# Up product of an MLP: new order of the first two column pairs, new makers of their split operands, and two projections that take all attention heads at once

## The chip, the cores and the metric

The kernel runs on one core of a Trainium2 chip. The metric is the device time of one launch in microseconds (us), the median of several runs. The engines of a core work beside each other, each through a queue of its own in a fixed order: TensorE (PE, matmuls), VectorE (DVE), ScalarE (ACT), GpSimd (POOL), and SyncE (SP), which issues most of the transfers (DMAs); POOL issues some too.

## The reference, cut to what matters

One layer of a decoder with 1024 tokens and model width 1024. The change lies between the end of the cross-attention and the first part of the MLP:

```
h += CrossAttn(RMSNorm(h), RMSNorm(mem))     # 4 heads of 256, then the projection w_xo (1024 x 1024)
h += W_down( relu(RMSNorm(h) @ W_up)^2 )     # hidden width 4096
```

## The kernel before, in words

Everything is kept transposed: a tile has 128 channels as partitions and the 1024 tokens as its free dimension. The hidden state h is eight such tiles, ht0 to ht7. Matmuls of float32 values are made of three: each operand is split in a high part (a rounded cast, made by ACT) and a low part (the value less its high part, made by DVE or POOL), and high x high, high x low and low x high are added up in PSUM. In the profile, `oh`/`ol` and `wh`/`wl` are such halves, and nearly every matmul has line L73, that of a helper.

**Projection of the attention.** The outputs of heads 0 and 1 are four split tiles, parts0; those of heads 2 and 3 are parts1. `project` (L1345) multiplies four of them with a 128-column piece of w_xo (24 matmuls into a PSUM tile `ps_g`, of which there are two) and DVE adds the result to an ht tile (L1350). Ahead of the MLP stage all eight tiles get the part of parts0 (L1360 to L1362), while the last pieces of the attention (`values`, PSUM tile `ps_xo`) are worked in between; work that is put off with `after` runs at `step` calls between matmuls, or all at once at `drain`.

**Stream tiles of the up product.** A stage of its own (L1404 to L1437) starts with the spread of the norm's factor over all partitions: DVE makes a diagonal matrix `hx_dg` (L242), PE multiplies it (`ps_bs`), ACT copies the result to `rbx`. Then for kp = 0 to 3 the tiles i = kp and kp + 4 get the projection of parts1, are written out (`d_h`, by SP), and are scaled into v (L1419). From the two v tiles, cut in halves of 512 tokens, seven stream operands of a Strassen-like scheme are made (x11, t1, t2, x21, x22, t3, t4), each split by `slice_of` (L1383) in a cast on ACT (L1386) and a subtraction on DVE (L1387). In the profile they are `blk`. They take memory that others leave, in the order that `spare` yields (L1368): of the split tiles of earlier stages, of the ht tiles, and at last of pool `opd`, tag `sl`, in which the v tiles, rbx and hx_dg lie (four places). `next` of a place whose tile is still read waits for its readers.

**The up product.** Class `Pair` (L1468): 16 pairs of column blocks of w_up, seven products for each instead of eight, 12 matmuls each (four k x three), 1344 in all, into PSUM tiles `ps_up` of a pool with four banks. `weights(j)` makes the stationary operand `st` of product j out of the loaded w_up tiles (`ws`) or sums of them (`s`, on DVE): a cast on ACT (L1449), a subtraction on POOL (L1450). `result` adds the products up: p1 is ACT's copy of product 1, u2 = p1 + product 6 (L1526), u5 = u2 + product 5 (L1529); product 7 is added to u2 in L1531, and the outputs r are u2 + product 5, u2 + product 4, u5 + product 3 and p1 + product 2, then squared where positive, and written out. The bank of product 5 is read for the last time after product 7.

Pairs 0 and 1 form the first group (L1545): (0,1), (0,5), (1,1), (1,5), then products 6, 2, 3, 7, 4 of pair 0, and the same of pair 1. In (pr, j), pr is the pair and j the product. The weights of a whole group are emitted ahead of its products, at high priority; each engine's final order is made by a scheduler from the emitted order and these priorities. Behind the up product stands the down product (`ps_d`).

Of the kernel before, what the change touches and what calls it, by code (L numbers as in the profile page):

```python
# [17 lines left out]
P = 128  # L18
# [37 lines left out]
def trunk_kernel(tc, w_io):  # L56
# [3 lines left out]
    with ctx:  # L60
# [1144 lines left out]
        with ExitStack() as sc:  # L1205
# [136 lines left out]
                ):  # L1342
                    after(start + at, lambda fn=fn, args=args: fn(*args))

            def project(parts, slot, i2, j):  # L1345
                wh, wl = last_slot[0] = slot
                cols = lambda w, k: w[:, k * 256 + j * P:k * 256 + j * P + P]
                ps = gemm_ch(lambda k: (cols(wh, k), cols(wl, k)), hi(parts), lo(parts), 4, T)
                hv = ht[i2 * 2 + j]
                dve.tensor_add(hv, hv, ps)  # L1350

            last_slot = [None]
            parts0 = [pair(opb) for _ in range(4)]
            parts1 = []
            for h in range(4):
# [1 line left out]
                if h == 3:  # L1357
                    parts1 += [pair(opa) for _ in range(4)]
                attend(h, qT, parts0[h * 2:] if h < 2 else parts1, h % 2 * 2 if h > 1 else 0, 8)
            for i2 in range(4):  # L1360
                project(parts0, wslot(w_io["w_xo"][0, i2]), i2, 0)
                project(parts0, last_slot[0], i2, 1)  # L1362
            drain()

        def spare():  # L1368

            for pool_, tags, n in ((opc, ("oh", "ol"), 4), (opb, ("oh", "ol"), 4), (opd, ("sl",), 1)):  # L1370
                for tag in tags:
                    for _ in range(n):
                        yield pool_, tag
            for i in (0, 4, 1, 5, 2, 6, 3, 7):
                yield hp, f"ht{i}"
            for _ in range(3):
                yield opd, "sl"

        opd = ctx.enter_context(tc.tile_pool(name="opd", bufs=4))
        spares = spare()  # L1380
        blocks = {}

        def slice_of(name, src):  # L1383
            pool_, tag = next(spares)
            t = pool_.tile([P, 2, 512], F32R, tag=tag, name="blk")
            act.copy(t[:, 0, :], src)  # L1386
            dve.tensor_sub(t[:, 1, :], src, t[:, 0, :].bitcast(F32))  # L1387
            blocks.setdefault(name, []).append(t)

        f = []  # L1390
# [13 lines left out]
        with ExitStack() as sc:  # L1404
# [5 lines left out]
            for kp in range(4):  # L1410
                if kp % 2 == 0:
                    slots = [wslot(w_io["w_xo"][1, kp // 2 + 2 * q]) for q in range(2)]
                vs = []
                for q in range(2):
                    i = kp + 4 * q
                    project(parts1, slots[q], i // 2, kp % 2)
                    nc.sync.dma_start(d_h[i], ht[i])
                    v = opd.tile([P, T], F32, tag="sl", name="v")
                    dve.scalar_tensor_tensor(v, ht[i], C("g_mlp", i), rbx, ALU.mult, ALU.mult)  # L1419
                    vs.append(v)  # L1420
                    lo_, hi_ = v[:, :512], v[:, 512:]
                    if q == 0:
                        slice_of("x11", lo_)
                        t1 = mp.tile([P, 512], F32, tag="p1", name="t1", bufs=2)
                        dve.tensor_sub(t1, hi_, lo_)
                        slice_of("t1", t1)
                t2 = mp.tile([P, 512], F32, tag="u2", name="t2")
                t3 = mp.tile([P, 512], F32, tag="u5", name="t3")
                b12, (b21, b22) = vs[0][:, 512:], (vs[1][:, :512], vs[1][:, 512:])
                dve.tensor_sub(t2, b22, t1)  # L1430
                slice_of("t2", t2)
                slice_of("x21", b21)
                slice_of("x22", b22)
                dve.tensor_sub(t3, b22, b12)
                slice_of("t3", t3)
                dve.tensor_sub(t2, b21, t2)
                slice_of("t4", t2)  # L1437

            nstat = [0]

            def stationary(src):

                n = nstat[0] % 10
                nstat[0] += 1
                if n < 6:
                    t = wp.tile([P, 2, 512], F32R, tag=("wh", "wl")[n % 2], name="st")
                else:
                    t = opa.tile([P, 2, 512], F32R, tag="oh", name="st")
                act.copy(t[:, 0, :], src)  # L1449
                pool.tensor_sub(t[:, 1, :], src, t[:, 0, :].bitcast(F32))  # L1450
                return t

            def squares_of(i):
# [14 lines left out]
            class Pair:  # L1468


                def __init__(self, pr):
                    self.pr, self.a, self.st, self.banks = pr, [], {}, {}
# [33 lines left out]
                def product(self, j):  # L1506
                    ps = self.banks[j] = pss.tile([P, 512], F32, tag="s", name="ps_up")
# [8 lines left out]
                            step()  # L1516
                    self.result(j, ps)

                def result(self, j, ps):
                    seen, banks = self.banks, self.banks  # L1520
                    if j == 1:
                        self.p1 = mp.tile([P, 512], F32, tag="p1", name="p1", bufs=2)
                        act.copy(self.p1, ps)
                    if j in (1, 6) and 1 in seen and 6 in seen:
                        self.u2 = mp.tile([P, 512], F32, tag="u2", name="u2")
                        dve.tensor_add(self.u2, self.p1, banks[6])  # L1526
                    if j in (5, 6) and 5 in seen and 6 in seen:
                        self.u5 = mp.tile([P, 512], F32, tag="u5", name="u5")
# [17 lines left out]
            groups += [[(pr, j) for j in ORDER] for pr in range(2, 16)]  # L1546
            for group in groups:
                pairs = {}
                with tc.high_priority():
                    for pr, j in group:  # L1550
                        if pr not in pairs:
                            pairs[pr] = Pair(pr)
                        pairs[pr].weights(j)
                for pr, j in group:
                    if j == ORDER[0] and 2 <= pr < 10:
# [3 lines left out]
                    pairs[pr].product(j)  # L1559
            drain()  # L1560

        if True:
# [173 lines left out]
```

## Time and profile before

| | |
|---|---|
| median of 3 runs | 2715.16 us (2714.44 to 2717.03) |
| the profiled execution | 2716.95 us |
| its span in the trace | 2715.2 us |
| mean granted clock of TensorE in it | 0.995 of full speed |

The profile has a page with busy shares, and answers to queries of the trace: waits of an engine by what released it, timelines (start, duration, engine, line, operation, output tile <- input tiles, shapes, count; in square brackets the idle time before it and what ended it), groups of instructions, and windows with the clock that the throttle granted to TensorE. Neighbouring instructions of one kind stand as one row with a count. Matmuls are pipelined: the next starts before the last has ended. A matmul of 128x512 lasts about 0.39 us in these rows.

### The profile page before, as it was taken

Reading aid. Unit: us, or ns where it says so; the run is one execution under the profiler, and the core shown is the slowest. Engines: PE = TensorE matmul, PEld = TensorE weight load, DVE = VectorE, ACT = ScalarE, POOL = GpSimd, SP = SyncE. Lnnn points to the kernel's source line nnn. Section 1 sums busy time; section 2 is a strip of 40 time slices with the busy share of each in tenths; the row PEclk is TensorE's granted clock in tenths of the full one; section 3 lists DMA queues with packets and bytes.
Section 4 is the critical chain, followed back from the end, with each engine's and each line's share of the span. In section 5 each row is a group of like instructions: output and inputs, shape, how many; then the busy total and the mean of one; then the engine's idle time right before and its main releaser. Section 6 shows DMA issues by size and latency. Waiting matters only on the chain. (4 is left out here: it accounts for less than half of the span.)

```text
span 2715.2 us, 31722 instructions
## 1 busy us (share of the span) xinstructions
PE 2681.2 (99%) x12368; PEld 2164.6 (80%) x12368; DVE 1605.4 (59%) x1887; ACT 1074.0 (40%) x1749; POOL 794.6 (29%) x442
## 2 busy tenths in 40 slices
PE   9999999999999999999999999999998999999999
PEld 7888878888787878775588778888876888888887
DVE  7598878758666776524414773434568886532423
ACT  6533321225666656556612351324423332222221
POOL 2332221200505050414342432321115664422220
PEclk9999999999999999999999999999999999999999
DMA  7642232344555555672444332311123332454642
GB/s 249 204 131 95 96 114 88 122 125 86 148 155 148 142 146 154 179 228 76 140 178 155 117 109 93 101 58 32 59 85 109 147 132 109 179 187 140 207 134 70
DMA packets 119574, 354.79 MB, mean 131 GB/s; under 512 B 12016, under 2 KB 37120, under 8 KB 119040
## 3 DMA queue, kind: packets, MB, share of 16 engines
q1 hardware_dynamic: 112656, 328.12, 35.8%
q0 software_dynamic: 6768, 24.64, 5.4%
q8 instruction: 97, 1.59, 0.2%
q14 instruction: 53, 0.43, 0.1%
HBM read 277.06 MB, written 78.80 MB: 131 GB/s over the span
## 5 line engine op out<-in xcount | busy, mean ns | idle before, releaser
L73 PE MATMUL ps_g<-oh,wh 128*128 128x512 f32 x1872 | 604.3, 403 | 9.1 <-ACT oh L267 3.9
L73 PE MATMUL ps_g<-ol,wh 128*128 128x512 f32 x1872 | 591.8, 394 | 3.0 <-DVE ol L268 2.8
L73 PE MATMUL ps_g<-oh,wl 128*128 128x512 f32 x1872 | 582.1, 391 | 1.5 <-POOL wl L168 1.5
L168 POOL TENSOR_TENSOR wl<-ws,wh 128x1024 fp32r<-128x1024 f32 (+2 forms) x106 | 261.9, 2472 | 714.7 <-ACT wh L162 682.6
L73 PEld LDWEIGHTS ps_g<-ol,wh 128*128 128x128 f32 x1872 | 351.8, 188 | 89.3 <-issue 9.3
L73 PEld LDWEIGHTS ps_g<-oh,wl 128*128 128x128 f32 x1872 | 352.2, 188 | 77.2 <-POOL wl L168 1.9
L73 PEld LDWEIGHTS ps_g<-oh,wh 128*128 128x128 f32 x1872 | 339.0, 189 | 73.0 <-issue 5.5
L362 DVE SCALAR_TENSOR_TENSOR tapy<-hin,cst,tapy 128x1024 f32<-128x1024 f32 x240 | 354.6, 1477 | 32.7 <-ACT tapy L357 26.2
L162 ACT CAST wh<-ws 128x1024 fp32r<-128x1024 f32 (+1 forms) x169 | 176.4, 1044 | 466.9 <-PE ps_g L73 303.1
L73 PE MATMUL ps_up<-blk,st 128*128 128x512 f32 x1344 | 310.0, 393 | 8.8 <-DVE blk L1387 5.7
L73 PEld LDWEIGHTS ps_up<-blk,st 128*128 128x128 f32 x1344 | 254.3, 190 | 63.8 <-DVE blk L1387 6.3
L268 DVE TENSOR_TENSOR ol<-r_in,oh 128x1024 fp32r<-128x1024 f32 x64 | 91.7, 1437 | 222.8 <-ACT oh L267 222.8
L73 PE MATMUL ps_d<-ol,wh 128*128 128x512 f32 x512 | 199.5, 390 | 0.4 <-DVE ol L268 0.2
L73 PE MATMUL ps_d<-oh,wl 128*128 128x512 f32 x512 | 199.2, 389 | 0.0
L73 PE MATMUL ps_d<-oh,wh 128*128 128x512 f32 x512 | 199.2, 389 | 0.0
L73 PE MATMUL ps_tm<-wh,oh 128*128 128x512 f32 x448 | 175.8, 393 | 0.4 <-DVE zth L637 0.4
L73 PE MATMUL ps_tm<-wh,ol 128*128 128x512 f32 x448 | 174.6, 390 | 0.0
L73 PE MATMUL ps_tm<-wl,oh 128*128 128x512 f32 x448 | 174.4, 389 | 0.0
L166 POOL DMA_DIRECT2D wl<-w_ch x45 | 39.1, 868 | 378.6 <-ACT wl L165 378.6
L182 POOL TENSOR_TENSOR wl<-ws,wh 128x1024 fp32r<-128x1024 f32 x28 | 76.3, 2736 | 218.1 <-ACT wh L181 218.0
L267 ACT CAST oh<-r_in 128x1024 fp32r<-128x1024 f32 x64 | 67.2, 1053 | 180.1 <-PE ps_d L73 173.0
L791 DVE SCALAR_TENSOR_TENSOR c4a<-c4v,cst,c4a 128x1023 f32<-128x1023 f32 (+2 forms) x72 | 96.6, 1341 | 59.5 <-ACT c4a L789 48.4
(388 smaller groups left out, 3843.6 us busy)
## 6 DMA issues: line engine op xcount, KB each, us to landing
r_in<-d_r SPq DMA_DIRECT2D x64, 512.0 KB, 3.7
ws<-w_ch SPq DMA_DIRECT2D x63, 512.0 KB, 3.5
wl<-w_ch POOLq DMA_DIRECT2D x45, 512.0 KB, 5.8
csb<-d_cs SPq DMA_DIRECT2D x32, 512.0 KB, 4.0
gth<-d_th SPq DMA_DIRECT2D x32, 512.0 KB, 4.4
ws<-w_up SPq DMA_DIRECT2D x32, 512.0 KB, 3.3
d_r<-r SPq DMA_DIRECT2D x32, 512.0 KB, 2.6
ws<-w_down SPq DMA_DIRECT2D x32, 512.0 KB, 3.3
```

Of the source, the lines that this page charges most:

```text
L73: ins = nc.tensor.matmul(*a, **k)
L162: act.copy(wh[:, a:b], st[:, a:b])
L166: pool.dma_start(wl[:, a:b], src[:, a:b], accum_op=ALU.add)
L168: (low or pool).tensor_sub(wl[:, a:b], st[:, a:b], wh[:, a:b].bitcast(F32))
L182: pool.tensor_sub(wl[:, :, c], s3, wh[:, :, c].bitcast(F32))
L267: act.copy(a, src)
L268: dve.tensor_sub(b, src, a.bitcast(F32))
L362: dve.scalar_tensor_tensor(y, hin[:, j:j + T], w(j), y, ALU.mult, ALU.add)
L791: dve.scalar_tensor_tensor(a[:, s:], v[:, :T - s], C("c4_w", ct * 4 + 3 - s), a[:, s:], ALU.mult, ALU.add)
```

## The change

`project` takes a list of weight slots and a tile number, and runs over four or eight parts. Ahead of the MLP stage only the tiles 2 to 7 get the part of parts0; tiles 0 and 1 get one projection over parts0 and parts1 together in the MLP stage (`take`), and so one addition on DVE instead of two. The stage takes the tiles in the order 0, 4, 1, 5, 2, 3, 6, 7. The low parts of x21 and x22 are made by `added`: ACT writes the negated high part, and an accumulating transfer issued by POOL adds the value. The same makes the low parts of the stationaries 1, 2 and 4 of pairs 0 and 1; their stationaries 3, 5, 6 and 7 get theirs from DVE instead of POOL. For k = 3, t2 and t3 lie in a tile of their own (`t23`), and the two sums of pair 1 in another (`sums2`). Head order: (0,1), (0,5), (1,1), (1,5), then products 6, 7, 2, 3, 4, each for pair 0 and pair 1; their weights are emitted eight products ahead.

```diff
-            def project(parts, slot, i2, j):
-                wh, wl = last_slot[0] = slot
-                cols = lambda w, k: w[:, k * 256 + j * P:k * 256 + j * P + P]
-                ps = gemm_ch(lambda k: (cols(wh, k), cols(wl, k)), hi(parts), lo(parts), 4, T)
-                hv = ht[i2 * 2 + j]
-                dve.tensor_add(hv, hv, ps)
+            def project(parts, slots_, i):
+                cols = lambda w, k: w[:, k % 4 * 256 + i % 2 * P:k % 4 * 256 + i % 2 * P + P]
+                n = len(parts)
+                ps = pg.tile([P, T], F32, tag="g", name="ps_g")
+                steps = gemm_steps(lambda k: [cols(w, k) for w in slots_[k // 4]], hi(parts), lo(parts), n, ps)
+                for k in range(n):
+                    if k == 4:
+                        drain()
+                    next(steps)
+                    next(steps)
+                    step()
+                dve.tensor_add(ht[i], ht[i], ps)
...
-            for i2 in range(4):
-                project(parts0, wslot(w_io["w_xo"][0, i2]), i2, 0)
-                project(parts0, last_slot[0], i2, 1)
-            drain()
+            for i2 in range(1, 4):
+                slot = wslot(w_io["w_xo"][0, i2])
+                for i in range(2):
+                    project(parts0, [slot], i2 * 2 + i)
...
-            for pool_, tags, n in ((opc, ("oh", "ol"), 4), (opb, ("oh", "ol"), 4), (opd, ("sl",), 1)):
+            for pool_ in (opc, opb):
...
-            for i in (0, 4, 1, 5, 2, 6, 3, 7):
+            for i in (0, 4, 1, 5, 2, 3, 6):
                 yield hp, f"ht{i}"
-            for _ in range(3):
-                yield opd, "sl"
+            for n in range(5):
+                yield (hp, "ht7") if n == 2 else (opd, "sl")
...
+        def added(t, src):
+            act.activation(t[:, 1, :], t[:, 0, :].bitcast(F32), AF.Copy, scale=-1.0)
+            pool.dma_start(t[:, 1, :], src, accum_op=ALU.add)
...
             act.copy(t[:, 0, :], src)
-            dve.tensor_sub(t[:, 1, :], src, t[:, 0, :].bitcast(F32))
+            if name in ("x21", "x22"):
+                added(t, src)
+            else:
+                dve.tensor_sub(t[:, 1, :], src, t[:, 0, :].bitcast(F32))
...
+            def take(i):
+                if i // 2 not in slots:
+                    slots[i // 2] = wslot(w_io["w_xo"][1, i // 2])
+                if i < 2:
+                    project(parts0 + parts1, both + [slots[0]], i)
+                else:
+                    project(parts1, [slots[i // 2]], i)
+                nc.sync.dma_start(d_h[i], ht[i])
+                vs[i] = v = opd.tile([P, T], F32, tag="sl", name="v")
+                dve.scalar_tensor_tensor(v, ht[i], C("g_mlp", i), rbx, ALU.mult, ALU.mult)
...
+            for k in range(2):
+                upper(k)
+                take(k + 4)
+                t2, t3 = temps()
+                second(k, t2)
+                third(k, t3)
+                plain([k])
+                fourth(k)
+            upper(2)
+            upper(3)
+            take(6)
+            t2, t3 = temps()
+            second(2, t2)
+            third(2, t3)
+            take(7)
+            t23 = xr.tile([P, T], F32, tag="acc", name="t23")
+            second(3, t23[:, :512])
+            third(3, t23[:, 512:])
+            plain([2, 3])
+            fourth(2)
+            fourth(3)
...
                 act.copy(t[:, 0, :], src)
-                pool.tensor_sub(t[:, 1, :], src, t[:, 0, :].bitcast(F32))
+                if early and plain:
+                    added(t, src)
+                else:
+                    (dve if early else pool).tensor_sub(t[:, 1, :], src, t[:, 0, :].bitcast(F32))
...
-                    self.st[j] = stationary(src)
+                    self.st[j] = stationary(src, self.pr < 2, j in (1, 2, 4))
...
-            groups = [[(0, 1), (0, 5), (1, 1), (1, 5)] + [(pr, j) for pr in range(2) for j in (6, 2, 3, 7, 4)]]
...
+            head = [(0, 1), (0, 5), (1, 1), (1, 5)] + [(pr, j) for j in (6, 7, 2, 3, 4) for pr in range(2)]
+            with tc.high_priority():
+                pairs = [Pair(pr) for pr in range(2)]
+                for pr, j in head[:8]:
+                    pairs[pr].weights(j)
+            for i, (pr, j) in enumerate(head):
+                with tc.high_priority():
+                    pairs[pr].product(j)
+                    if i + 8 < len(head):
+                        pairs[head[i + 8][0]].weights(head[i + 8][1])
```

`upper(k)` takes tile k and makes its x11 and t1; `second`, `third` and `fourth` make t2, t3 and t4, `plain` x21 and x22, as the loop of before did. In the changed program the cast of `slice_of` has line L1398 and its subtraction L1402, the negation and the transfer of `added` L1392 and L1393, v L1439, t2, t3 and t4 L1450, L1454 and L1463, the stationaries' subtraction L1506, the sums of w_up tiles L1543, L1545 and L1547, and u2 L1591.

How this moves instructions is shown at two places. First TensorE's order from the attention's last product (`ps_xo`, heads 2 and 3) to the spread (`ps_bs`). Before the change (48 matmuls of two projections, of which the last three rows are shown, and then 6 of the first projection in the MLP stage, `ps_g_14233`):

```order
L73 MATMUL ps_g_14185<-oh_12868,wh_14155 128x512 x2
L73 MATMUL ps_g_14185<-ol_12869,wh_14155 128x512 x2
L73 MATMUL ps_g_14185<-oh_12868,wl_14156 128x512 x2
L73 MATMUL ps_g_14233<-oh_13770,wh_14223 128x512 x2
L73 MATMUL ps_g_14233<-ol_13771,wh_14223 128x512 x2
L73 MATMUL ps_g_14233<-oh_13770,wl_14224 128x512 x2
L73 MATMUL ps_bs_14241<-hx_dg_14220,mat_73 128x512
```

And with the change, where `ps_g_14175` is the projection of tile 0 over all heads:

```order
L73 MATMUL ps_xo_14143<-xpTh_14092,xvl_13783 128x512
L73 MATMUL ps_g_14175<-oh_12862,wh_14165 128x512 x2
L73 MATMUL ps_g_14175<-ol_12863,wh_14165 128x512 x2
L73 MATMUL ps_g_14175<-oh_12862,wl_14166 128x512 x2
L73 MATMUL ps_bs_14183<-hx_dg_14162,mat_73 128x512
L73 MATMUL ps_bs_14186<-hx_dg_14162,mat_73 128x512
L73 MATMUL ps_g_14175<-oh_12864,wh_14165 128x512 x2
```

The spread stands 6 matmuls behind `ps_xo` now, where 54 stood between them.

Second VectorE's order from the scaling of the last tile to the first sum of products (`u2` = p1 + product 6 of pair 0). Before, where `s` are sums for the next pair's weights:

```order
L1419 SCALAR_TENSOR_TENSOR v_14574<-ht7_10261,cst_72,rbx_14219 128x1024
L1489 TENSOR_TENSOR s_14886<-s_14884,ws_14880 128x512
L1430 TENSOR_TENSOR t2_14576<-v_14574,t1_14542 128x512
L1387 TENSOR_TENSOR blk_14585<-v_14574,blk_14585 128x512
L1387 TENSOR_TENSOR blk_14582<-v_14574,blk_14582 128x512
L1387 TENSOR_TENSOR blk_14579<-t2_14576,blk_14579 128x512
L1491 TENSOR_TENSOR s_14897<-ws_14880,ws_14882 128x512
L1434 TENSOR_TENSOR t3_14577<-v_14574,v_14537 128x512
L1436 TENSOR_TENSOR t2_14576<-v_14574,t2_14576 128x512
L1387 TENSOR_TENSOR blk_14589<-t3_14577,blk_14589 128x512
L1387 TENSOR_TENSOR blk_14593<-t2_14576,blk_14593 128x512
L1526 TENSOR_TENSOR u2_14729<-p1_14673,ps_up_14716 128x512
```

With the change, from v of the last tile on, and behind the rows left out the t3 slice of k = 3 (`blk_14572`), three sums for pair 2 (`ws_14888`, `ws_14890`), and the t4 slices of k = 2 and 3 (`blk_14592`, `blk_14596`):

```order
L1439 SCALAR_TENSOR_TENSOR v_14564<-ht7_10261,cst_72,rbx_14161 128x1024
L1506 TENSOR_TENSOR st_14714<-s_14630,st_14714 128x512
L1450 TENSOR_TENSOR t23_14566<-v_14564,t1_14487 128x512
...
L1402 TENSOR_TENSOR blk_14572<-t23_14566,blk_14572 128x512
L1543 TENSOR_TENSOR s_14892<-ws_14890 128x512
L1545 TENSOR_TENSOR s_14894<-s_14892,ws_14888 128x512
L1547 TENSOR_TENSOR s_14905<-ws_14888,ws_14890 128x512
L1402 TENSOR_TENSOR blk_14592<-u2_14527,blk_14592 128x512
L1402 TENSOR_TENSOR blk_14596<-t23_14566,blk_14596 128x512
L1591 TENSOR_TENSOR u2_14730<-p1_14658,ps_up_14717 128x512
```

The subtractions for x21 and x22 are gone from VectorE; the first sum of products stands behind the last t4 slice as before, and behind three sums of pair 2's weights, whose second load of w_up goes into the place of `ws_14601`.

More of the change, by code (lines that the diff above doesn't have):

```diff
@@ L1409, in trunk_kernel @@
             after(0, lambda: spread(xr, rx[0], T, "hx", rbx, dg))
[L1410 to L1430, printed above, removed]
@@ new lines, in trunk_kernel @@
+            slots = {}
+            vs, t1s, t2s = {}, {}, {}
+            both = [wslot(w_io["w_xo"][0, 0])]
+            def take(i):
[8 more added lines that the diff above has]
+                dve.scalar_tensor_tensor(v, ht[i], C("g_mlp", i), rbx, ALU.mult, ALU.mult)
@@ L1431, in trunk_kernel, with upper, second @@
+            def upper(k):
+                take(k)
+                slice_of("x11", vs[k][:, :512])
+                t1s[k] = mp.tile([P, 512], F32, tag="p1", name="t1", bufs=2)
+                dve.tensor_sub(t1s[k], vs[k][:, 512:], vs[k][:, :512])
+                slice_of("t1", t1s[k])
+            def second(k, t2):
+                t2s[k] = t2
+                dve.tensor_sub(t2, vs[k + 4][:, 512:], t1s.pop(k))
                 slice_of("t2", t2)
-                slice_of("x21", b21)
-                slice_of("x22", b22)
@@ L1434, in trunk_kernel, with third, plain, fourth @@
-                dve.tensor_sub(t3, b22, b12)
+            def third(k, t3):
+                dve.tensor_sub(t3, vs[k + 4][:, 512:], vs.pop(k)[:, 512:])
                 slice_of("t3", t3)
-                dve.tensor_sub(t2, b21, t2)
-                slice_of("t4", t2)
+            def plain(ks):
+                for h in range(2):
+                    for k in ks:
+                        slice_of(("x21", "x22")[h], vs[k + 4][:, h * 512:h * 512 + 512])
+            def fourth(k):
+                dve.tensor_sub(t2s[k], vs.pop(k + 4)[:, :512], t2s[k])
+                slice_of("t4", t2s.pop(k))
@@ new lines, in temps @@
+            def temps():
+                return [mp.tile([P, 512], F32, tag=tag, name=tag) for tag in ("u2", "u5")]
+            for k in range(2):
[12 more added lines that the diff above has]
+            third(2, t3)
@@ L1439, in trunk_kernel, with stationary @@
+            take(7)
[5 more added lines that the diff above has]
+            fourth(3)
             nstat = [0]
-            def stationary(src):
+            def stationary(src, early, plain):
                 n = nstat[0] % 10
@@ L1471, in __init__ @@
                 def __init__(self, pr):
-                    self.pr, self.a, self.st, self.banks = pr, [], {}, {}
+                    self.pr, self.a, self.st, self.banks, self.sums2 = pr, [], {}, {}, None
                     for q in range(2):
@@ L1517, in product, with sum_of @@
                     self.result(j, ps)
+                def sum_of(self, tag):
+                    if self.pr != 1:
+                        return mp.tile([P, 512], F32, tag=tag, name=tag)
+                    if self.sums2 is None:
+                        self.sums2 = xr.tile([P, T], F32, tag="acc", name="sums2")
+                    o = 512 if tag == "u5" else 0
+                    return self.sums2[:, o:o + 512]
                 def result(self, j, ps):
@@ L1524, in result @@
                     if j in (1, 6) and 1 in seen and 6 in seen:
-                        self.u2 = mp.tile([P, 512], F32, tag="u2", name="u2")
+                        self.u2 = self.sum_of("u2")
                         dve.tensor_add(self.u2, self.p1, banks[6])
                     if j in (5, 6) and 5 in seen and 6 in seen:
-                        self.u5 = mp.tile([P, 512], F32, tag="u5", name="u5")
+                        self.u5 = self.sum_of("u5")
                         dve.tensor_add(self.u5, self.u2, banks[5])
@@ L1544, in trunk_kernel @@
             ORDER = (6, 1, 5, 7, 2, 3, 4)
-            groups = [[(0, 1), (0, 5), (1, 1), (1, 5)] + [(pr, j) for pr in range(2) for j in (6, 2, 3, 7, 4)]]
-            groups += [[(pr, j) for j in ORDER] for pr in range(2, 16)]
-            for group in groups:
-                pairs = {}
-                with tc.high_priority():
[L1550 to L1555, printed above, removed]
+            head = [(0, 1), (0, 5), (1, 1), (1, 5)] + [(pr, j) for j in (6, 7, 2, 3, 4) for pr in range(2)]
[4 more added lines that the diff above has]
+            for i, (pr, j) in enumerate(head):
+                with tc.high_priority():
+                    pairs[pr].product(j)
+                    if i + 8 < len(head):
+                        pairs[head[i + 8][0]].weights(head[i + 8][1])
+            for pr in range(2, 16):
+                with tc.high_priority():
+                    now = Pair(pr)
+                    for j in ORDER:
+                        now.weights(j)
+                for j in ORDER:
+                    if j == ORDER[0] and pr < 10:
                         squares_of(pr - 2)
@@ L1558, in trunk_kernel @@
                         after(0, factor)
-                    pairs[pr].product(j)
+                    now.product(j)
             drain()
```

5 lines of the change are left out of this document (2 added, 3 removed).

## The prediction

> **What bounds the kernel now.** The page first.
>
> ```profile
> span 2715.2 us, 31722 instructions
> PE 2681.2 (99%) x12368; PEld 2164.6 (80%) x12368; DVE 1605.4 (59%) x1887; ACT 1074.0 (40%) x1749; POOL 794.6 (29%) x442
> ```
>
> TensorE (PE) is busy for 2681.2 of 2715.2 us. The change leaves the number of matmuls as it is: 16 projections of 24 matmuls before, 12 of 24 and 2 of 48 after, 384 both times, and the same 1344 of the up product. So only two things can move the time: where PE waits, and how fast it is clocked around a wait. The waits by releaser come next.
>
> ```profile
> PE ps_up L73 <- DVE blk L1387: 5.7, 2, 4.4
> PE ps_up L73 <- ACT blk L1386: 3.2, 2, 1.9
> PE ps_g L73 <- DVE ht L1350: 2.6, 1, 2.6
> ```
>
> Five waits, 11.5 us in all, lie in the part that is rewritten: one in the projections, four at the start of the up product, all for stream tiles that VectorE (DVE) and ScalarE (ACT) have not finished. The timeline of PE gives their places, and the windows of PE the clock granted behind them (last columns: busy, count, PEclk, DMA share, GB/s).
>
> ```profile
> 2023.15 0.70 PE L73 MATMUL ps_g<-oh,wh 128*128 128x512 f32 x2 [2.63 <-DVE ht L1350]
> 2039.59 2.20 PE L73 MATMUL ps_up<-blk,st 128*128 128x512 f32 x9
> 2043.74 0.49 PE L73 MATMUL ps_up<-blk,st 128*128 128x512 f32 x1 [1.95 <-ACT blk L1386]
> 2048.59 4.50 PE L73 MATMUL ps_up<-blk,st 128*128 128x512 f32 x11 [4.36 <-DVE blk L1387]
> 2054.30 0.49 PE L73 MATMUL ps_up<-blk,st 128*128 128x512 f32 x1 [1.21 <-ACT blk L1386]
> 2056.12 54.15 PE L73 MATMUL ps_up<-blk,st 128*128 128x512 f32 x231 [1.32 <-DVE blk L1387]
> 2199.64 40.74 PE L73 MATMUL ps_up<-blk,st 128*128 128x512 f32 x179
> ```
> ```profile
> 1336.20:1340.90 4.70, 4.65 (x14) 0.50 0.82 273
> 2048.50:2053.20 4.70, 4.50 (x11) 0.60 0.16 40
> 2056.10:2059.00 2.90, 2.88 (x7) 0.50 0.93 287
> 2059.00:2062.00 3.00, 3.00 (x15) 0.98 0.00 0
> ```
>
> One matmul starts (40.74 - 0.39) / 178 = 0.2267 us after the last, where 0.39 is the pipelined last one. Eleven then take 2.66 us; behind the 4.36 us wait they took 4.50, at clock 0.60: 1.84 lost. 231 take 52.53; they took 54.15: 1.6 lost, at clock 0.50 until about 2059. An idle time is counted from the end of a matmul (0.39), the pace from its start (0.2267), so each of the five waits costs 0.16 more than it shows, 0.8 in all. The place costs 11.5 + 3.4 + 0.8 = **15.7 us**, and that is all that this change can win.
>
> **What it removes.** DVE is the engine that PE waited for. These rows of its timeline give the pace there: 0.60 us from one 128x512 operation to the next, 1.20 for the scaling v (2034.44 to 2035.64), 1.13 for an addition of a projection (2035.64 to 2036.77).
>
> ```profile
> 2034.44 1.27 DVE L1419 SCALAR_TENSOR_TENSOR v<-ht,cst,rbx 128x1024 f32<-128x1024 f32 x1
> 2035.64 1.21 DVE L1350 TENSOR_TENSOR ht<-ht,ps_g 128x1024 f32<-128x1024 f32 x1
> 2036.77 0.68 DVE L1430 TENSOR_TENSOR t<-v,t 128x512 f32<-128x512 f32 x1
> ...
> 2040.88 0.68 DVE L1436 TENSOR_TENSOR t<-v,t 128x512 f32<-128x512 f32 x1
> 2041.48 1.27 DVE L1419 SCALAR_TENSOR_TENSOR v<-ht,cst,rbx 128x1024 f32<-128x1024 f32 x1
> ```
>
> Off DVE go 8 subtractions for x21 and x22 and two 1.13 us additions, 8 x 0.6 + 2 x 1.13 = 7.1 us; onto it come 8 subtractions for stationaries, 4.8. What matters more is the order: the operands of (0,1), (0,5), (1,1), (1,5), which are x11 and t1 alone, are made before anything of the last lower tiles. I placed the new order of each engine by hand, instruction behind instruction, with the durations quoted here; the same walk over the old order gives its five waits as 2.21, 2.32, 4.23, 1.07 and 1.64, 11.5 in all. In the new order the last x11/t1 slice is done near 2036.5, before the up product starts. All five old waits go.
>
> **New wait 1, at the spread (1.7 us).**
>
> ```profile
> 1980.46 0.63 PE L73 MATMUL ps_g<-oh,wh 128*128 128x512 f32 x2
> 1980.66 2.81 DVE L242 TENSOR_TENSOR hx_dg<-mat,hx_r 128x1024 f32<-128x1024 f32 x1 [0.16 <-PE ps_xo L73]
> 1992.75 1.88 PE L73 MATMUL ps_bs<-hx_dg,mat 128*128 128x512 f32 x4
> ```
>
> Today two projections lie between the last product of the attention (it ends at 1980.46, and hx_dg starts behind it) and ps_bs, which reads hx_dg. Behind the change only 6 matmuls do, 1.36 us. PE is ready at 1981.82, hx_dg at 1980.66 + 2.81 = 1983.47 (PE's order is strict: everything waits with ps_bs): 1.65, say 1.7. If hx_dg runs at its usual 1.2 instead, 0.1; the row has POOL's 2.39 us wl beside it, and it stays beside it.
> From 1983.5, ps_bs with what runs beside it takes 1.32 (1992.75 to 1994.07), and the other 234 of the 240 projection matmuls from there on (2 x 48 + 6 x 24) take 53.05: the up product starts at **2037.9** instead of 2039.59.
>
> **New wait 2, small, at (0,6).** The last load of w_up that DVE's order needs follows the last weight conversion of the projections and lands, by the walk, at 2017.3. From there DVE has no gap: 30 short operations, 5 additions and 5 scalings, 30 x 0.605 + 5 x 1.13 + 5 x 1.20 = 29.8, so the last v (tile 7) ends at 2047.1 to 2047.4, and t2 of k=3, cast and subtracted, some 4 us later at 2051.4. The first four products take 48 x 0.2267 = 10.9, to 2048.8; (0,6) gets to its k=3 at 2051.0. Wait: 0.4.
>
> **New wait 3, at (0,7): the term that decides.** There are four PSUM banks. (0,1) and (1,1) free theirs by ACT's copy; (0,5) and (1,5) keep theirs for the sums. So (0,6) and (1,6) take the last two, and (0,7) can only start when DVE has read (0,6) in the addition u2 (L1591). The rows of DVE's order (shown ahead) put this addition behind the two t4 subtractions. Their tiles lie in the memory of v of tiles 6 and 7, which the accumulating transfers of x21 and x22 read. So: last v 2047.4, ACT then has 13 operations that start 0.52 apart,
>
> ```profile
> 2025.60 1.14 ACT L1386 CAST blk<-v 128x512 fp32r<-128x512 f32 x2
> 2026.64 0.62 ACT L1386 CAST blk<-t 128x512 fp32r<-128x512 f32 x1
> ```
>
> until the last negation (2054.3), POOL issues the last transfer at 2054.7, it lands L later, then ACT's cast 0.6, the subtraction and the addition, 3.8 with the gaps: the bank comes free at 2058.5 + L. (By DVE's load of pair 2, which waits for the landing of the (0,4) stationary's transfer, it would be 2057.4 + L.) PE is ready at 2037.9 + 72 x 0.2267 + 0.4 = 2054.6. What is L, for 256 KB accumulated on POOL's queue? No row has this very transfer. Nearest rows:
>
> ```profile
> wl<-w_ch POOLq DMA_DIRECT2D x45, 512.0 KB, 5.8
> d_yc<-oT SPq DMA_DIRECT2D x16, 256.0 KB, 2.4
> DMA to landing us min/median/max: 5.2/6.0/9.5
> q0 software_dynamic: 6768, 24.64, 5.4%
> ```
>
> The first and third are accumulating transfers of POOL of twice the size (5.2 to 9.5); the second is 256 KB without an accumulation, on SyncE's queue. I take **L = 5**, a little under the fastest and median 512 KB ones, which are nearest in kind; ends 2.4 and 9.5. The bank then comes free at 2063.5: a wait of **8.9 us** (6.3 and 13.4 at the ends).
> The Trainium skill, "DMA: Bandwidth & Descriptors", section "Anatomy of one DMA — SWDGE (gpsimd) path", fits 2.0 us + bytes/436e3 per transfer, an estimate of 2.6 for 256 KB, by which the sum would end 2.4 us earlier; but for 512 KB it gives 3.2 where the row has 5.8, so the trace does not bear it out here.
> After 8.9 us idle the clock will be low for a few us, as behind 3.92 us at 1336.2 (0.50) and at 2056.1: the two losses seen are 1.84 and 1.6, so **2.0**.
>
> **Sum.** From 2056.12 to the end of the up product today:
>
> ```profile
> L73 PE MATMUL ps_up<-blk,st x1344: 387/389/797, 2039.6 to 2361.2; 128*128 128x512 f32 x192
> ```
>
> 1322 matmuls in 305.1 us, of which 1.6 is the clock loss above: 303.5 without it, and 50 fewer matmuls are 11.3 less, so the 1272 from (0,7) on take 292.2. New end: 2063.5 + 292.2 + 2.0 = 2357.7 against 2361.2, **-3.5**. I add 0.8, since the walk puts the last v of the old order at 2040.6 where the trace has 2041.48: **-2.7**. By losses it is the same: 15.7 goes, 1.7 + 0.4 + 8.9 + 2.0 = 13.0 comes. Behind the up product the order is as it was. From the profiled execution's 2716.95 us that gives 2714.2; the median of the runs shown, 2715.16, lies 1.8 below that execution, so I predict **2712.5**.
>
> What the accumulating transfers cost beside this: each holds POOL for its issue only,
>
> ```profile
> 645.57 0.86 POOL L166 DMA_DIRECT2D wl<-w_ch  x1 [12.77 <-ACT wl L165]
> 644.82 2.60 DVE L362 SCALAR_TENSOR_TENSOR tapy<-hin,cst,tapy 128x1024 f32<-128x1024 f32 x2
> ```
>
> 0.86 us beside two undisturbed DVE operations (v above, of the same operation and size, took 1.27), 14 of them where POOL has little else. The negations on ACT that are late are among its 13 above; the earlier ones belong to slices that are done when PE comes for them.
> A rule speaks against the change: the Trainium skill, "SBUF — State Buffer", box 'The "DVE blocks DMA" trap (SWDGE)', has POOL's descriptors starved beside certain DVE operations, 3100 ns for a transfer of 620. Its 2.5 us on L would make the sum -0.2. The row above does not show it: the issue was not stretched.
>
> **Rivals.**
> *The wait at (0,7) does not arise* (the tiles or the bank are free earlier than I read). Then 15.7 goes and 2.1 comes: -13.6, **2701.6**. Against it: the addition would have to be through by 2054.6, and even with L = 0 it is 2058.5. For it: my reading of memory reuse may miss a free place.
> *Fast landing.* L of 2.4 to 3.8 makes -5.3 to -3.9 and with an undisturbed hx_dg another -1.5: **2708 to 2710.5**. For it the 2.4 of SyncE's queue; against it that this is another queue without a read of its target.
> *The transfers go one behind another* (the slower side). Eight are issued from 2042 on, before the last. If each took its full 6.0 us with the next behind it, the last lands near 2042 + 8 x 6.0 = 2090 instead of 2060: 30 us more of wait on -2.7, **2742**. It decides for slower by over 5.4 us once L of the last is above 13, that is from 3.2 us each in series. Against it: queue q0 moved 24.64 MB (47 transfers of 512 KB) in 5.4% of 2715.2 us = 147 us, 3.1 us each of all 16 engines, 1.6 for 256 KB, and the walk issues the eight between 2042.2 and 2054.7, 1.8 apart.
> *The change doesn't do what it says*: the order shows that it does; DVE's rows put every operand of the first four products ahead. No chance of its own.
>
> **Chances.** The forecast with its bounds 0.58, fast landing 0.19, no wait 0.14, series 0.09. A measurement of this kernel can tell about 0.2%, 5.4 us, from no change, so faster means below 2709.7: all of no wait, half of fast landing, and 0.04 of the forecast (no clock loss), 0.28. Slower means above 2720.6: series and 0.02 of the forecast (DVE later by over 8 us), 0.11. Same: 0.61. The range goes from 2706.5 (fast landing with both gains and a little of the clock) to 2719.0 (L = 9.5 makes +1.8, 2717.0, and 2 us more for drift on DVE); it leaves out no wait, and series.
>
> **What would show it.** In the new trace: ps_bs behind a wait of about 1.7 for hx_dg; the first ps_up at about 2038 with no wait in its first 48 matmuls; a wait of 7 to 13 us for L1591 at the 73rd; the last transfer of L1393 landing at about 2060; clock near 0.5 for 3 us behind it. Wrong would be: a longer first ps_up (the projections behind the spread starved of weights), t2 late by more than 2 us at (0,6), or the 73rd matmul without a wait.

## The result, and the profile after

The changed kernel takes 2720.56 us (median of 22 runs) against 2716.64 us of the kernel before (22 runs on the same chip). The ratio of the runs is 1.0014, with a 95% interval of 1.0007 to 1.0020: 3.8 us longer (1.9 to 5.4), which is small, but clear of no change, since the interval does not reach 1. One of the 22 runs took 7161.23 us, far off all others; the ratio is taken without it. The forecast was 2.7 us shorter, and its range ended at 2719.0.

The profiled execution of the changed kernel took 2724.19 us. Its waits of TensorE by releaser (total, times, longest), those of them that lie in the part of the change:

```profile
PE ps_up L73 <- DVE u L1591: 12.6, 1, 12.6
PE ps_bs L73 <- DVE hx_dg L242: 1.5, 1, 1.5
PE ps_d L73 <- DVE r L1603: 1.3, 1, 1.3
PE ps_up L73 <- ACT blk L1398: 1.2, 1, 1.2
```

The five old waits of 11.5 us are gone. 1.5 us at the spread, 1.4 at a t2 slice (with 0.2 that the list above doesn't show), 1.3 at the down product and 12.6 in one place stand instead. TensorE's timeline at the head of the up product:

```profile
1986.55 1.98 PE L73 MATMUL ps_bs<-hx_dg,mat 128*128 128x512 f32 x4 [1.49 <-DVE hx_dg L242]
...
2041.51 13.08 PE L73 MATMUL ps_up<-blk,st 128*128 128x512 f32 x57
2055.76 0.50 PE L73 MATMUL ps_up<-blk,st 128*128 128x512 f32 x1 [1.17 <-ACT blk L1398]
2056.49 3.51 PE L73 MATMUL ps_up<-blk,st 128*128 128x512 f32 x14 [0.23 <-DVE blk L1402]
2072.62 196.61 PE L73 MATMUL ps_up<-blk,st 128*128 128x512 f32 x858 [12.62 <-DVE u L1591]
```

The first four products and the start of (0,6) run without a gap (57 matmuls), the k=3 slice of t2 costs 1.17 + 0.23, and the 73rd matmul, (0,7), waits 12.62 us. Behind it the clock is low once more:

```profile
2072.60:2075.60 3.00, 2.98 (x7) 2.41 (x8) 2.36 (x4) 0.00 (x0) 0.00 (x0) 0.50 0.00 0
```

At the pace of 0.2267 us, 858 matmuls would take 857 x 0.2267 + 0.39 = 194.67; they took 196.61, so 1.94 went there.

To compare the two traces, three points of TensorE serve: the last product of the attention (ps_xo), the first and the last of the up product. Rows of the tile views, before and after (first and last start at the end of each row):

```profile
L73 PE MATMUL ps_xo<-xpTh,xvh x32: 387/390/398, 1851.1 to 1979.8; 128*128 128x512 f32 x32
```
```profile
L73 PE MATMUL ps_xo<-xpTh,xvh x32: 387/390/397, 1854.2 to 1982.8; 128*128 128x512 f32 x32
L73 PE MATMUL ps_up<-blk,st x1344: 387/389/796, 2041.5 to 2366.7; 128*128 128x512 f32 x192
```

| stretch, us | before | after | difference |
|---|---|---|---|
| last ps_xo to first ps_up | 59.8 | 58.7 | -1.1 |
| first to last ps_up | 321.6 | 325.2 | +3.6 |
| last ps_up to the end of the span (2715.2, 2722.3) | 354.0 | 355.6 | +1.6 |

Together +4.1, close to the 3.8 of the timed runs. The other 3 us between the two spans lie ahead of the change: the first ps_xo of this row already starts 3.1 us later.

### The profile page after: what moved, and what is told of

It reads as the page before. It is cut to its first block, busy times and chain, and to the rows that moved or that the text cites. A ratio compares the mean times of both kernels' runs of the same rounds, so it can differ in the third digit from the quotient of the medians.

```text
span 2722.3 us, 31762 instructions
## 1 busy us (share of the span) xinstructions
PE 2681.9 (99%) x12368; PEld 2164.8 (80%) x12368; DVE 1599.7 (59%) x1885; ACT 1081.6 (40%) x1763; POOL 779.9 (29%) x442
## 3 DMA queue, kind: packets, MB, share of 16 engines
q8 instruction: 97, 1.59, 0.2%
## 4 chain that ended last, share of the span: by engine, by line
PE 87%; DVE 5%; issue 4%; DMA 2%; ACT 1%; POOL 1%; SPq 0%; ACTq 0%; DVEq 0%; POOLq 0%
PE ps_g L73 42%; PE ps_d L73 12%; PE ps_up L73 10%; PE ps_tm L73 9%; PE ps_yd L73 2%; PE ps_kv L73 2%; PE ps_lg L73 1%; PE ps_pt L77 1%; PE ps_xl L73 1%; PE ps_yo L73 1%; PE ps_stt L73 1%; PE ps_xo L73 1%; PE ps_xq L73 1%; PE ps_o L73 1%; DVE ol L268 1%
## 5 line engine op out<-in xcount | busy, mean ns | idle before, releaser
L73 PE MATMUL ps_up<-blk,st 128*128 128x512 f32 x1344 | 308.5, 391 | 14.0 <-DVE u L1591 12.6
```

The lines of the kernel that those rows point to most:

```text
L73: ins = nc.tensor.matmul(*a, **k)
```

## The experiments

Each is the changed kernel with the edit named. Times are medians beside those of the kernel before on the same chip (2717.27 for runs 1 to 4, 2717.71 for 5 to 8, 2716.85 for 9 and 10); the changed kernel itself stands at 1.0014.

| | ratio to before, 95% | median, us | first to last ps_up, us |
|---|---|---|---|
| 1 stationaries of product 4 by DVE | 1.0000 (0.9991 to 1.0009) | 2716.80 | 322.0 |
| 2 late x21, x22 by DVE | 0.9968 (0.9956 to 0.9979) | 2707.90 | 313.6 |
| 3 sums in the output tiles | 0.9994 (0.9985 to 1.0003) | 2714.53 | 320.0 |
| 4 spread later | 1.0016 (1.0007 to 1.0024) | 2721.85 | 325.5 |
| 5 no transfers | 1.0003 (0.9994 to 1.0012) | 2719.69 | 321.6 |
| 6 banks, shared tile | 1.0020 (1.0012 to 1.0029) | 2723.46 | 327.8 |
| 7 edits 2, 3 and 4 | 0.9962 (0.9949 to 0.9974) | 2707.78 | 313.5 |
| 8 as 7, but x21, x22 of k=2 by transfers | 0.9970 (0.9959 to 0.9980) | 2709.25 | 315.7 |
| 9 banks apart | 0.9994 (0.9985 to 1.0003) | 2715.65 | 319.9 |
| 10 as 7, and edit 1 | 0.9969 (0.9957 to 0.9980) | 2708.56 | 315.2 |

What held u2 (L1591) back is read from DVE's timeline of the changed kernel:

```profile
2057.08 0.68 DVE L1402 TENSOR_TENSOR blk<-t,blk 128x512 fp32r<-128x512 f32 x1
2067.68 0.69 DVE L1543 TENSOR_TENSOR s<-ws 128x512 f32<-128x512 f32 x1 [9.91 <-DMA ws<-w_up]
2068.40 0.69 DVE L1545 TENSOR_TENSOR s<-s,ws 128x512 f32<-128x512 f32 x1
2069.01 0.68 DVE L1547 TENSOR_TENSOR s<-ws 128x512 f32<-128x512 f32 x1
2069.61 0.68 DVE L1402 TENSOR_TENSOR blk<-u,blk 128x512 fp32r<-128x512 f32 x1
2070.22 1.75 DVE L1402 TENSOR_TENSOR blk<-t,blk 128x512 fp32r<-128x512 f32 x1
2071.89 0.68 DVE L1591 TENSOR_TENSOR u<-p,ps_up 128x512 f32<-128x512 f32 x1
```

DVE stands idle for 9.91 us ahead of a sum for pair 2, until the load of w_up lands. In the chain of waits the three links ahead are:

```profile
2055.50 6.95 DMA st<-ws
2062.46 0.04 issue
2062.50 5.15 DMA ws<-w_up
2067.68 0.70 DVE s L1543
```

The accumulating transfer of the (0,4) stationary reads the place of the new load, the load waits for its landing, the sum for the load, and u2, which stands behind the sum in DVE's order, for the sum. A second chain ends not much earlier: the landing of x22 (ACT's cast starts at 2066.83 behind it) and the t4 slice. The first experiments part the two.

**1. The stationaries of product 4 from DVE.**

```diff
-                    self.st[j] = stationary(src, self.pr < 2, j in (1, 2, 4))
+                    self.st[j] = stationary(src, self.pr < 2, j in (1, 2))
```

> The stationaries of (0,4) and (1,4) get their low part from DVE instead of a transfer; all else as changed. In the changed kernel the wait of 12.62 us at (0,7) ends with DVE's u2, which stands behind the sum s (L1543) that waited until 2067.68 for the second load of w_up of pair 2, whose place is read by the (0,4) transfer. Theory A (this load decides): the load starts some 6 us earlier, and the next chain takes over, the x22 transfer of k=2, whose landing at 2065.1 frees the memory of a t4 slice: wait at (0,7) 5 to 8 us, time 4 to 7 us below the changed kernel. Theory B (the x22 transfers and the memory decide by themselves): wait 11 to 13, time within 1.5 us of the changed kernel.

```profile
2062.20 0.69 DVE L1543 TENSOR_TENSOR s<-ws 128x512 f32<-128x512 f32 x1 [4.87 <-DMA ws<-w_up]
2068.97 41.21 PE L73 MATMUL ps_up<-blk,st 128*128 128x512 f32 x173 [9.93 <-DVE u L1591]
```

The wait fell by 2.7 us, to 9.93, between the ranges of the two theories (5 to 8, and 11 to 13). The time fell by about 0.14%, 3.8 us; its interval overlaps that of the changed kernel, so the trace says more here: the up product takes 322.0 us instead of 325.2. The load now landed at 2062.2, and DVE went on at once; but it was held again, 1.55 us by a POOL subtraction ahead of another sum and 1.06 by a t4 slice that took 1.75 us, so u2 came at 2068.2 only. The landings of x22 (ACT's cast behind the first at 2064.67) were close behind too. So the load was the last link, as theory A had it, but the gain ended at the next links, sooner than it said.

**2. The late x21 and x22 from DVE.**

```diff
-            if name in ("x21", "x22"):
+            if name in ("x21", "x22") and len(blocks.get(name, [])) < 2:
```

> x21 and x22 of k=2 and 3 get their low part from DVE again (four subtractions more there, four transfers fewer); k=0 and 1 as changed. DVE's order then has u2 of pair 0 ahead of the sum that waits for w_up, and u2 of pair 1 behind it. Theory A (the load decides): (0,7) waits 1 to 3 us for DVE's longer work, and the wait for the load moves to (1,7), 1 to 4 us: together 3 to 6 instead of 12.6, time 6 to 9 below the changed kernel. Theory B (the transfers of the slices decide alone): no wait for a load, together under 2.5, time 10 to 13 below.

```profile
2063.57 0.69 DVE L1543 TENSOR_TENSOR s<-ws 128x512 f32<-128x512 f32 x1 [2.06 <-DMA ws<-w_up]
2060.96 3.03 PE L73 MATMUL ps_up<-blk,st 128*128 128x512 f32 x12 [0.34 <-DVE u L1591]
2064.92 6.01 PE L73 MATMUL ps_up<-blk,st 128*128 128x512 f32 x24 [0.93 <-DVE sums L1591]
```

This made the largest difference: 0.9968 of the kernel before, 8.7 us shorter, and some 12 below the changed kernel. The waits are A's places (a little at (0,7), the load's at (1,7)), but smaller than A said, and the time is that of B. A had left out that the load would land earlier with four transfers fewer around it: DVE waited for it until 2063.57 instead of 2067.68. Of the clock loss at most 0.4 us is left (24 matmuls in 6.01 us instead of 5.60), and the wait behind the up product went too.

**3. The sums in the tiles of their outputs.** u2 and u5 of pairs 0 and 1 are made in the halves of r that product 4 and product 3 complete later (`place` gives half 0 of the second output tile, and half 1 of the first).

```diff
-                        self.u2 = self.sum_of("u2")
+                        self.u2 = self.place("u2", 1, 0)
...
-                        self.u5 = self.sum_of("u5")
+                        self.u5 = self.place("u5", 0, 1)
```

> The sums u2 and u5 of pairs 0 and 1 lie in the tiles of their outputs, not in the memory of t2 and t3, so they need not wait for the t4 slices; DVE's order then has both u2 ahead of the sum that waits for w_up. Theory A (the load decides): (0,7) and (1,7) no longer wait, but the bank for (0,2) comes from the addition of product 7, which stands behind that sum: a wait of 4 to 7 us at (0,2), time 6 to 9 below the changed kernel. Theory B (only the memory of the t4 slices holds u2 back): no wait over 2 us in the up product's head, time 12 to 15 below.

```profile
2051.72 8.91 PE L73 MATMUL ps_up<-blk,st 128*128 128x512 f32 x38 [0.23 <-DVE blk L1402]
2066.51 4.51 PE L73 MATMUL ps_up<-blk,st 128*128 128x512 f32 x12 [5.88 <-DVE r L1603]
```

As A had it: 38 matmuls without a wait, to the end of (1,7), then 5.88 us at (0,2) for the addition of product 7, which DVE had behind the sum that waits for w_up (7.45 us, until 2063.37). The time is 0.20% below the changed kernel, 5.4 us, a little under the 6 to 9 of theory A; a wait of 2.7 us at the down product takes part of the gain back. The load's chain decides without any help of the memory.

**4. The spread later.**

```diff
-            after(0, lambda: spread(xr, rx[0], T, "hx", rbx, dg))
+            after(3, lambda: spread(xr, rx[0], T, "hx", rbx, dg))
```

> The spread of the norm's factor is put off by three steps of the first projection, so that 24 matmuls instead of 6 stand ahead of ps_bs; all else as changed. The wait of 1.49 us for hx_dg goes. Theory A: the loads and DVE behind it follow TensorE, so all comes earlier by it: 1 to 2 us below the changed kernel. Rival: DVE and the transfers do not come earlier, and the wait at (0,7) grows by what is won: within 0.5 us of the changed kernel.

```profile
2069.08 41.23 PE L73 MATMUL ps_up<-blk,st 128*128 128x512 f32 x172 [12.85 <-DVE u L1591]
```

The trace has no wait for hx_dg, 57.0 us from ps_xo to the up product instead of 58.7, and 12.85 us at (0,7) where there were 12.62. By the trace it is theory A; the timed ratio, 1.0016 against 1.0014, can't show 1.5 us. It stays open whether it is worth anything in the time.

**5. The order alone.**

```diff
-            if name in ("x21", "x22"):
+            if False:
...
-                if early and plain:
+                if False:
...
-                    (dve if early else pool).tensor_sub(t[:, 1, :], src, t[:, 0, :].bitcast(F32))
+                    pool.tensor_sub(t[:, 1, :], src, t[:, 0, :].bitcast(F32))
```

> The new order with the old makers: the low parts of x21 and x22 all come from DVE, those of the stationaries of pairs 0 and 1 from POOL, and no accumulating transfer is left. Theory A (the order is the gain, the transfers the loss): u2 of pair 0 does not wait for a load or a landing for long, the head of the up product waits 3 to 7 us in all, time 6 to 10 us below the kernel before. Rival (the order pays only with the new makers): POOL's subtractions stretch DVE's operations beside them from 0.69 to 1.75 us and the tiles are late as before, waits of 9 to 12 us, time within 3 us of the kernel before.

```profile
2029.78 0.70 PE L73 MATMUL ps_g<-oh,wh 128*128 128x512 f32 x2 [2.65 <-ACT st L1502]
2056.84 0.50 PE L73 MATMUL ps_up<-blk,st 128*128 128x512 f32 x1 [3.00 <-ACT blk L1398]
2068.04 42.24 PE L73 MATMUL ps_up<-blk,st 128*128 128x512 f32 x176 [5.07 <-DVE u L1591]
```

The rival was right: 1.0003 of before. With these three and 0.30 at another slice the waits come to 11 us, at other places than before, and 1.5 us at the spread and 1.0 at the down product come on top. In the same trace DVE operations of 0.68 us take up to 1.77 near POOL's subtractions, as the rival said. So the new order is worth nothing by itself; it needs some of the new makers, though not the late transfers (run 2). Which of them it needs was not tried.

**6 and 9. More PSUM banks.** In 6 the products 7 and 2 of pairs 0 and 1 go to the idle tiles of the projections, two halves to a tile; in 9 only (0,7) and (1,7), a tile each; the lines are those of run 9.

```diff
+                    if self.pr < 2 and j == 7:
+                        ps = pg.tile([P, T], F32, tag="g", name="ps_up")[:, :512]
...
```

> As changed, but the products 7 and 2 of pairs 0 and 1 go to the four PSUM banks of the projections, which are idle there; DVE's order keeps u2 behind the sum that waits for w_up and behind the t4 slices. Theory A (the bank of (0,6) is what TensorE waited for): no wait at (0,7), and 1 to 4 us at (0,3), whose bank comes free at the old time of about 2072.6; time 9 to 12 us below the changed kernel. Rival (an operand, st or blk, is late by itself and the bank only comes last): a wait of over 5 us at (0,7) or (0,2) that ends with a stationary or a slice; time less than 6 below.

> The banks once more: as changed, but the products (0,7) and (1,7) each go to an idle PSUM tile of the projections, a whole one each, so that neither shares a tile with another product. Theory A (a bank is what TensorE waits for, and u2 of pair 0 is what frees it): no wait at (0,7) and (1,7), which then run in the idle time; the wait moves to (0,2), which needs the bank of (0,6) at the old time, 24 matmuls or 5.4 us later: 6 to 8 us there, time 4 to 7 us below the changed kernel. Rival (something else holds TensorE until u2): the wait of 12 to 13 us stays at (0,7).

In run 6, (0,7) ran without a wait, as theory A has it, but (1,7) waited 13.91 us for the addition that reads (0,7), since the two share a tile:

```profile
2077.52 7.19 PE L73 MATMUL ps_up<-blk,st 128*128 128x512 f32 x24 [13.91 <-DVE u L1601]
```

So it missed its time, and run 9 takes the tiles apart:

```profile
2052.68 8.91 PE L73 MATMUL ps_up<-blk,st 128*128 128x512 f32 x38 [0.23 <-DVE blk L1402]
2069.02 41.22 PE L73 MATMUL ps_up<-blk,st 128*128 128x512 f32 x173 [7.42 <-DVE u L1595]
```

12 + 12 matmuls run in the old idle time, and the wait is 7.42 us at (0,2), where 12.62 less 24 x 0.2267 would be 7.2. All operands of (0,7) and (1,7) were there; a bank was what TensorE waited for.

**7, 8 and 10. The edits together.**

> Three edits at once: x21 and x22 of k=2 and 3 by DVE (as in the second experiment), the sums in the tiles of their outputs (third), the spread three steps later (fourth). Of the second experiment's waits, 1.49 at ps_bs goes, and 0.93 for the sum of (1,6), since u2 no longer stands behind a t4 slice. If TensorE sets the time of what follows: 2 to 3 us below the second experiment, 10 to 12 below the kernel before. Rival (DVE's work from the last projections on sets it, as the fourth experiment suggests): the waits at (0,6) and (0,7) grow by what is won, and it stays within 1 us of the second experiment.

> As the run of three edits, but x21 and x22 of k=2 stay with transfers, so DVE has two subtractions (1.2 us) fewer and two transfers are left in the cluster. If DVE sets the time: 0.5 to 1.5 us below the run of three edits. If the cluster of transfers does (the second load of w_up of pair 2 lands later, and the t4 slice of k=2 waits for a landing ahead of the second sum): 1 to 3 us above it.

> The run of three edits, and the stationaries of (0,4) and (1,4) by DVE as in the first experiment: no accumulating transfer is issued within 8 us of the cluster's place but those of two early stationaries, at the price of two more subtractions (1.2 us) ahead of u2. If what is left of the waits is DVE's work: 0.5 to 2 us above the run of three edits. If it is the last load of w_up, which lands at 2058.4 there: 0.5 to 2 us below it.

Run 7 is 0.9962 of before, the shortest here (2707.78 us), but its interval overlaps those of 2, 8 and 10, so the times don't rank them. By its trace the wait at the spread is gone (57.0 to the up product), and the up product takes 313.5 as in run 2, so the rival's shift to (0,6) and (0,7) is not seen; a wait of 0.96 us at the down product takes most of the rest back.

In 8, with two late transfers left, the up product takes 2.2 us more than in 7, and in 10, where DVE has two more subtractions, 1.7 us more. These are the matmuls behind the k=3 slice of t2 in 7, 8 and 10:

```profile
2052.25 6.21 PE L73 MATMUL ps_up<-blk,st 128*128 128x512 f32 x26 [0.77 <-DVE blk L1402]
2051.43 10.52 PE L73 MATMUL ps_up<-blk,st 128*128 128x512 f32 x38 [0.51 <-DVE blk L1402]
2056.07 4.89 PE L73 MATMUL ps_up<-blk,st 128*128 128x512 f32 x14 [1.35 <-DVE blk L1402]
```

At the pace of 0.2267 us they would take 6.06, 8.78 and 3.34: 0.15, 1.74 and 1.55 us are lost. The granted clock there is 1.00 in 7, 0.58 and 0.56 in 8 (2052 to 2056), and 0.50 in 10 (2056 to 2058). So most of both differences is a low clock behind the wait at (0,6). The waits of TensorE in the up product add up to 3.9 us in 7, 4.5 in 8 and 4.0 in 10: the late transfers cost 0.65 us more wait, and DVE's extra work moves the waits to (0,6) (2.9 us instead of 1.65) without lengthening them in all. That is too little, from one trace each, to say which maker is best; the times show only that all four runs are shorter than both kernels.

## Why the prediction was wrong

**Right, with their sizes:** the wait at the spread (1.7 said, 1.49 seen, 1.65 with the 0.16 that an idle time hides); the four first products without a wait; the head of the up product earlier than before (1.1 us by ps_xo, where 1.7 was said); the place that decides, (0,7), for a bank that u2 (L1591) frees; the clock behind it (2.0 said, 1.94 seen). Runs 9 and 3 show the bank and DVE's order behind it by experiment.

**Wrong: the size of that wait.** The step that failed is "New wait 3", where it takes "L = 5" for one transfer and sets the load's chain, "2057.4 + L", aside as the shorter one. By it the bank would have come free at 2057.4 + 5 = 2062.4. In the trace the up product starts 3.6 us later than in the walk (2041.51 against 2037.9), so 2066.0; it came free at 2071.89 + 0.68, 2072.6. Of the 6.6 us between, these make 6.4:

- the last v ended at 2052.49, where the walk shifted by 3.6 has 2051.0, and ACT's work behind it leads to the issue of the (0,4) transfer: 1.5;
- the (0,4) transfer took 6.95 us instead of 5: 1.95;
- the load of w_up behind it, for which the prediction names no time, took 5.15 us instead of 3.3, the median over all 32 loads before: 1.85;
- the second t4 slice took 1.75 us instead of 0.69, beside POOL's subtraction of 1.59 us that starts at 2069.82: 1.06.

```profile
ws<-w_up SPq DMA_DIRECT2D x32, 512.0 KB, 3.3
```
```profile
2069.82 1.59 POOL L1506 TENSOR_TENSOR st<-s,st 128x512 fp32r<-128x512 f32 x1 [7.32 <-ACT st L1502]
```

Run 1, where this chain is out of the way, still has 9.93 us at (0,7), near the 8.9 of the prediction, though other work holds it up there too (the 1.55 and 1.06 above). So the chain that the prediction followed would by itself have come near its figure; the one that it set aside ended last.

Two of the four are one mistake: transfer times were taken mostly from rows in which a transfer has the engines nearly to itself, and added to a walk in which eight accumulating transfers and four loads fall within 20 us. Of the first eleven accumulating 512 KB transfers of the kernel before, the two with a DMA share of 0.95 and 0.97 in the 6 to 7 us around and behind their issue took 6.9 and 6.7 us, the eight with 0.59 to 0.70 took 5.2 to 5.7, and one with 0.84 took 5.3. In the changed kernel the landing times by their place show the same: the first of the eight, issued at 2048.13, and the last six, from 2051 on (the second took 5.3); then the windows of all engines there (the last three columns are clock, DMA share and GB/s):

```profile
DMA to landing us min/median/max: 3.3/3.3/3.3
...
DMA to landing us min/median/max: 5.9/6.5/6.9
```
```profile
2049.50:2058.00 8.50, 7.10 (x31) 5.31 (x29) 7.39 (x11) 7.41 (x15) 3.50 (x5) 1.00 1.06 263
2058.00:2067.50 9.50, 2.00 (x9) 1.31 (x7) 0.00 (x0) 3.22 (x6) 3.46 (x4) 0.76 1.08 244
```

The transfer engines are busy throughout (a share of 1.06 and 1.08 by packet times), and a transfer of 256 KB that took 3.3 us at the start takes 5.9 to 6.9. The prediction's own bound (1.6 us of all engines for 256 KB, 1.8 us between issues) spoke of the accumulating transfers alone and left the loads beside them out. Run 2, with four transfers fewer, has 0.94 and 0.67 in these windows; its (0,4) transfer took 5.3 us instead of 6.95, the load behind it 3.3, and all four loads there 3.3 to 4.9.

```profile
2049.50:2058.00 8.50, 6.66 (x29) 4.97 (x28) 8.50 (x14) 6.76 (x14) 1.72 (x2) 1.00 0.94 242
2058.00:2067.50 9.50, 8.24 (x35) 6.14 (x34) 7.33 (x13) 3.36 (x6) 3.45 (x4) 1.00 0.67 171
```

So the transfers were neither in series, as the third rival had it, nor alone; they shared. The second rival, fast landing, had the lone transfer right (3.3 is in its 2.4 to 3.8), and the first, no wait, is the case that fell outright.

The Trainium skill, "DMA: Bandwidth & Descriptors", section "Anatomy of one DMA — SWDGE (gpsimd) path", has a fit that gives 2.6 us for 256 KB, an estimate; the lone ones here took 3.3 and those among the eight up to 6.95, so its figure would have made the error larger. The rule that spoke against the change, the Trainium skill, "SBUF — State Buffer", box 'The "DVE blocks DMA" trap (SWDGE)', is not what these traces show. The last two transfers were issued at 2059.14 and 2060.34, while DVE stood idle, and still took 5.9 and 6.4 us. In run 2 the (1,4) transfer, issued at 2058.22, took 3.4 us with DVE at work for 3.2 of them, and the (0,4) transfer 5.3 with DVE at work for 5.2; in the changed kernel the same transfer took 6.95 with DVE at work for 2.0.

**Wrong, smaller:** (0,6) waited 1.40 instead of 0.4, from the late v above; why v was late no run shows. By the prediction's own terms the 0.4 should have been 0.6, since TensorE comes to the k=3 slice at 2037.9 + 57 x 0.2267 = 2050.8. From the spread to the up product TensorE needed 55.0 us (1986.55 to 2041.51), where the walk adds 54.4, so its 2037.9 was 0.6 too early. And "Behind the up product the order is as it was" left out that DVE's order at its end is timed anew: TensorE waited 1.26 us for r there, behind an operation on r that took 2.89 us beside a POOL subtraction of 2.46.

```profile
2369.59 2.89 DVE L1604 SCALAR_TENSOR_TENSOR r<-r 128x512 f32<-128x512 f32 x1
```
```profile
2369.47 2.46 POOL L168 TENSOR_TENSOR wl<-ws,wh 128x1024 fp32r<-128x1024 f32 x1 [8.65 <-ACT wh L162]
```

The last stretch is 1.6 us longer; run 2 has none of it (354.0), and the other runs have 0.8 to 2.7 us of wait there. No run tested it by itself.

The sum closes. The walk said -3.5; the 0.8 that the prediction added to it stood for a late v, which the terms here hold already. (Its two sums, -3.5 by the walk and -2.7 by losses, met only through this 0.8, and 0.6 of it is the start that the walk has too early.) The start of the up product adds 0.6, (0,6) 1.3 (1.40 and twice 0.16, instead of 0.4), (0,7) 3.9 (12.62 + 0.16 instead of 8.9), the clock -0.1, the end 1.6: +3.8 in all, where the timed runs have 3.8 and the traces 4.1. That it meets the timed figure to the tenth is chance, as the two measures differ by 0.3.

## What to carry to other kernels

Where a change makes several transfers fall together, take their durations from a place as crowded as the one they go to, loads of other queues included, or widen the range: here they about doubled. A transfer that reads a buffer lengthens the life of that buffer: follow the next load into it, and then who stands behind the first user of that load in its engine's order. An instruction for the far future, here a sum for pair 2, can hold the near one behind it, and giving the near one its own memory or bank (5.88 and 7.42 us of wait left in runs 3 and 9) or taking the transfer out of the chain (9.93 in run 1) shortens the wait instead of ending it, as the next link then holds. Run 2, which thinned out the transfers themselves, left under 1 us at each of the places behind.

## What was not expected of the hardware

The 256 KB accumulating transfers slowed from 3.3 to 6.95 us beside each other and beside loads, and the loads from 3.3 to 5.15. A DVE operation of 0.69 us took 1.75 beside a POOL subtraction of 1.59, and one took 2.89 beside one of 2.46. And a short wait does not settle the clock: behind 1.65 us of idle time at (0,6) it stayed at 1.00 in run 7, behind 1.68 at the same place it fell to 0.58 in run 8, at a price of 1.7 us. Why, no run here shows.
